# Hybrid mLSTM, attention and Fourier trunk: the gates move behind the Fourier projection, adaLN products run two blocks at a time

## The chip, the cores and the metric

The kernel runs on 1 core of one Trainium2 chip. The metric is device time in microseconds, the median of 3 runs. TensorE is called PE here, with PEld for its weight loads; VectorE is DVE, ScalarE ACT, GpSimd POOL, and SP is the engine that issues most DMAs.

## The reference, cut to what matters

Two layers work on 512 tokens (256 of context, 256 latent) of width 1024 in float32. In each layer, adaLN makes six shift, scale and gate vectors from the condition; then a mixer with three branches and a feed-forward network follow.

```python
ml = split((silu(c) @ w_ada[l] + b_ada[l]), 6)          # the same for the context: mc
h = rmsnorm(x, norm_g[l, 0]) * (1 + ml[1]) + ml[0]
u = split_cols(h @ w_in[l])   # q, k, v, o of the mLSTM; 16 gate columns; q, k, v of the attention; Fourier; merge gates
i_f, f_f, i_b, f_b = split(u[4] + gate_b, 4)            # the mLSTM's gates, per head and direction
b = cumsum(log_sigmoid(f)); dmat = where(tri, b_t - b_s + i_s, -inf); m_t = max(b_t + m, max_s dmat)
a = exp(dmat - m_t) * (q @ k.T); den = sum(a) + ...; h_ml = num / max(|den|, exp(-m_t))
y = g0 * (h_ml @ w_br_ml) + g1 * (diff_attn @ w_br_da) + g2 * (fourier @ w_br_fn)
x = x + ml[2] * (y @ w_out);  x = x + ml[5] * swiglu(modulate(rmsnorm(x), ml[3], ml[4]))
```

The gates' part (`i`, `f`, the cumulative sums and the running maximum) depends only on 16 of the projection's columns. Its results are first needed in the mLSTM, which comes after the attention.

## The kernel before, in words

**Jobs.** `plan` writes each layer as a list of jobs. A job is a piece of a weight matrix of 512 KB (128 columns by 1024 rows, or 512 by 256), used by 24 matmuls of PE. `Job.load` fetches it on SP into one of 4 raw buffers (`wraw`). `Job.split` cuts it in a high and a low part of float32r, since each product is made of three: ACT writes the high part (L214), DVE the low one by a subtraction (L224). While job i runs, `run_all` has split up to job i + 3 and asked for loads up to job i + 7, as far as raw buffers are free. `proj_t` (L309 to L311) and `proj_n` (L330 to L332) are the two kinds of matmul loop. After every sixth or so of a job's matmuls they yield: four ticks a job.

**Sides.** `side(name, gen, steps, jobs)` lets a second piece of work run along: with each tick it advances by steps / (4 x jobs) steps. `drain(name)` runs what is left of it.

**The gate job** (`GateJob`, 16 columns in a tile of 128) is loaded by a memset of POOL (L231) and four small DMAs (L233), 4 columns each. Its low part is made by POOL (L222), not DVE. Its product goes to one of the four side banks of PSUM; other projections use the four main banks.

**The gates** (`ml_gates`) are a chain on 36 partitions by 512 columns: copies from PSUM (L1015, L1018), the logarithm of the sigmoid by a polynomial of degree 12 (L1024 to L1036), two scans (L1039, L1044), copies (L1054, L1056), eight transposes on PE (L1061), and a last copy and an exponential (L1065, L1066). Nearly all of it is on DVE. It advances in 16 steps.

**adaLN** (`Ada.steps`): each of five calls multiplies the condition with 1024 rows and 2048 columns of `w_ada`, in eight blocks of 128 rows. A block is loaded by two DMAs (L364) into two of the 32 units of SBUF (`unit()`), and takes four float32 products with 32 output columns, each on its own 32 columns of PE's array; in the trace they are eight L371. In step k the loads of block k are issued, and the products of block k - 2. Two of the calls (`adab`, `adac`) run along in each layer, a fifth (`ada1`) in layer 0's feed-forward part. The opening does the same kind of product on its own (L399), two blocks together.

**Order of a layer's first part.** In layer 0 an opening of four dk jobs in a hand-written order (`opening_jobs`), in layer 1 three dk jobs (`first_jobs`). Then the gate job; then the rest of dk and dq, with the sides `gates`, `adab` and, from dq on, `hf` (the folding of the activations for the Fourier branch, `fold_h`). A rotary embedding on DVE (L1214, L1215) and POOL (L1216) takes every dk and dq block out of PSUM. Then z, the Fourier projection (`proj_z`: 8 jobs with folded weights, L789 on DVE or POOL, and L836); then dv with the side `adac`; then q, k and v with the side `da`, the attention.

**What sets the order.** SP's order is that of the program. On the other engines a planner orders the instructions when the kernel is built: it plays the program through with its own costs and takes the earliest instruction of the text that it holds to be ready. Within the opening and the layers' boundaries the order is by hand on DVE and ACT, in the opening on PE and POOL too. On the chip each engine runs its list strictly in that order.

Of the kernel before, what the change touches and what calls it, by code (L numbers as in the profile page):

```python
# [18 lines left out]
KB = D // 128  # L19
# [7 lines left out]
CQ, CK, CV, CO, CGATE, CDQ, CDK, CDV, CZ, CG = 0, 1024, 2048, 3072, 4096, 4112, 5136, 6160, 7184, 8208  # L27
# [16 lines left out]
def tile_trunk(ctx: ExitStack, tc: tile.TileContext, x, c, cx, c_ctx, w_ada, b_ada, norm_g, w_in, ml_gate_b,  # L44
               ml_head_g, da_lam, da_head_g, w_br_ml, w_br_da, w_br_fn, w_out, w_ffn_in, w_ffn_out, final_g,
               consts, out):
    nc = tc.nc
    V, S, G, T = nc.vector, nc.scalar, nc.gpsimd, nc.tensor
# [13 lines left out]
    def nm(p):  # L62
        cnt[0] += 1
        return f"{p}_{cnt[0]}"

    def unit(dt=F32):
        return upool.tile([128, 2, 512], dt, tag="u4", name=nm("u"))
# [7 lines left out]
    def main_ps():  # L75
        return pm.tile([128, 512], F32, tag="m", name=nm("m"))

    def side_ps():
        return psd.tile([128, 512], F32, tag="s", name=nm("p"))
# [15 lines left out]
    s32 = cpool.tile([128, KB, 32], F32, tag="s32", name="s32")  # L95
# [89 lines left out]
    def act_k(acts, k, n0, n1):  # L185
        return acts[0][k // 2][:, k % 2, n0:n1], acts[1][k // 2][:, k % 2, n0:n1]

    def unit_n():
        return upool.tile([128, 4, 256], F32, tag="u4", name=nm("n"))
# [46 lines left out]
    def call(fn):  # L236
        prog.append(("call", fn))

    def side(name, gen, steps, jobs):
        prog.append(("side", name, gen, steps / (4.0 * jobs)))  # L240

    def drain(name):
        prog.append(("drain", name))
# [59 lines left out]
    def proj_t(src, acts, n0, evac, cls=Job):  # L303

        def run(job):
            ps = side_ps() if cls is GateJob else main_ps()
            for k in range(KB):
                ah, al = act_k(acts(), k, n0, NT)
                T.matmul(ps[:, n0:], lhsT=job.hi[:, k, :], rhs=ah, start=(k == 0), stop=False)  # L309
                T.matmul(ps[:, n0:], lhsT=job.hi[:, k, :], rhs=al, start=False, stop=False)  # L310
                T.matmul(ps[:, n0:], lhsT=job.lo[:, k, :], rhs=ah, start=False, stop=(k == KB - 1))  # L311
                if k == KB - 1:
                    evac(ps)
                if k % 2:
                    yield
        prog.append(cls(src, KB, 128, run))

    def proj_n(src, nk, acts, tbs, evac):

        st = {}  # L320

        def mk(kt):
            def run(job):
                if kt == 0:
                    st.update({tb: main_ps() for tb in tbs})
                for tb in tbs:
                    for j in range(2):
                        k = 2 * kt + j
                        ah, al = act_k(acts(), k, tb * 128, tb * 128 + 128)
                        T.matmul(st[tb], lhsT=ah, rhs=job.hi[:, j, :], start=(k == 0), stop=False)  # L330
                        T.matmul(st[tb], lhsT=ah, rhs=job.lo[:, j, :], start=False, stop=False)  # L331
                        T.matmul(st[tb], lhsT=al, rhs=job.hi[:, j, :], start=False, stop=(k == nk - 1))  # L332
                    if kt == nk // 2 - 1:
                        evac(tb, st[tb])
                    yield
            return run
        for kt in range(nk // 2):
            prog.append(Job(src[kt * 256:kt * 256 + 256, :], 2, 512, mk(kt)))


    class Ada:
# [12 lines left out]

        def steps(self):
            self.start()
            pend = []
            for k in range(KB + 2):
                if k < KB:
                    raws = []  # L360
                    for hf in range(2):
                        raw = unit()
                        c0 = 2048 * self.s + 1024 * hf
                        nc.sync.dma_start(raw.rearrange("p a n -> p (a n)"),  # L364
                                          w_ada[self.l, k * 128:k * 128 + 128, c0:c0 + 1024])
                        raws.append(raw)
                    pend.append(raws)
                if k >= 2:
                    raws = pend.pop(0)
                    for j in range(4):  # L370
                        T.matmul(self.ps[32 * j:32 * j + 32, :], lhsT=s32[:, k - 2, :], rhs=raws[j // 2][:, j % 2, :],  # L371
                                 start=(k == 2), stop=(k == KB + 1))
                yield
            self.rows = arow_pool()
            V.tensor_tensor(out=self.rows, in0=self.ps, in1=self.bias, op=ALU.add)
            if self.s > 0:
                self.scr = dpool.tile([2, 4, 512], F32, tag="ascr", name=nm("as"))
                for r in range(2):
                    nc.sync.dma_start(self.scr[r], self.rows[r:128:32, :])
# [37 lines left out]
    def arow_pool():  # L417
        return cpool.tile([128, 512], F32, tag="arow", name=nm("ar"), bufs=3)
# [914 lines left out]
    def plan(l, xget, fin, bd1, bd2, bdn):  # L1333
# [6 lines left out]
        W = w_in[l]  # L1340
        vc = {n: vcol[:, 32 * l + o:32 * l + o + 8] for n, o in VROW.items()}
        st = {"yd": ([], []), "ym": ([], []), "q": [], "k": [], "v": [], "dq": [], "dk": [], "dv": [],
              "ys": [], "yy": ([], []), "us": ([], []), "ox": []}
        nT = len(tbs)
        hf = []
# [12 lines left out]
        h = lambda: bd1().h  # L1358
# [17 lines left out]
        def proj_tt(key, c0, nn0, rot=False, b0=0):  # L1376
            for b in range(b0, 8):
                proj_t(W[:, c0 + b * 128:c0 + b * 128 + 128], h, nn0, evac_t(key, nn0, b, rot))

        def proj_nn(key, c0, tt, f):  # L1380
            for g in range(2):
                def evac(tb, ps, g=g):
                    if tb == tt[0]:
                        st[key] += [unit_n(), unit_n()]
                    for j in range(2):
                        f(st[key][2 * g + j][:, tb, :], ps[:, j * 256:j * 256 + 256], j)
                proj_n(W[:, c0 + g * 512:c0 + g * 512 + 512], KB, h, tt, evac)
# [63 lines left out]
            opening_jobs(bd1, specs, parts)  # L1451
        else:
            first_jobs(bd1, specs)
        proj_t(W[:, CGATE:CGATE + 16], h, 0, lambda ps: st.__setitem__("gps", ps), GateJob)
        call(start)
        side("gates", lambda: ml_gates(l, st["gps"], st), 18, 10)
        side("adab", ada[1].steps, 10, 10)
        proj_tt("dk", CDK, 0, True, nop)
        side("hf", lambda: fold_h(h(), len(segs), hf, st), 12 if l == 0 else 8, 7 * nT // 4)
        proj_tt("dq", CDQ, n0, True)  # L1460
        drain("gates")
        drain("adab")
        drain("hf")
        proj_z(l, W, len(segs), hf, st)
        side("adac", ada[2].steps, 10, 8)
        proj_nn("dv", CDV, ALL, cp)
        drain("adac")
        qjobs = 8 * nT // 4
        side("da", lambda: diff_attn(l, st, tbs), (8 * nT + 4) * 3, qjobs + 15)
# [135 lines left out]
    ctx.enter_context(tc.manual_schedule(engines={mybir.EngineType.SP}))  # L1605
    call(begin)
    plan(0, None, fin, bd[0], bd[1], bd[2])
    plan(1, lambda: fin[0], fin, bd[2], bd[3], bd[4])
    run_all()

# [55 lines left out]
```

## Time and profile before

| | |
|---|---|
| runs | 1986.34, 1986.89, 1986.90 us; median 1986.89 |
| profiled execution | 1987.21 us, span 1985.4 us |
| PE busy | 1923.4 us, 97% |
| DVE busy | 1195.1 us, 60% |
| ACT busy | 783.9 us, 39% |
| POOL busy | 147.0 us, 7% |
| DMA | 269.5 MB, mean 136 GB/s |
| mean granted clock | 0.992 |

Busy time is not time at the peak: matmuls overlap, and their ends are modelled. The time that counts for PE is from start to start. Layer 0's dk and dq stand at about 61 to 157 us of the span, its z at 157 to 182 and its dv at 182 to 236; in layer 1 dk and dq are at about 1243 to 1326, z at 1326 to 1342 and dv at 1342 to 1396.

### The profile page before, as it was taken

To read this page: it belongs to the slowest core of one execution; us is meant where nothing else is said; L and a number is where in the kernel's file an instruction comes from. 1 tells how busy PE (TensorE), PEld (TensorE's weight loads), DVE (VectorE), ACT (ScalarE), POOL (GpSimd) and SP (SyncE) were. 2 spreads that over 40 slices of the span, in tenths; PEclk is the share of its full clock that TensorE was granted. 3 is DMA by queue.
4 is the path that set the end of the run, shared out by engine and by line. 5 is a ranking of instruction groups with operands and counts; after the bars stand their busy time and mean duration, and the time that the engine had idled before them with its cause. 6 is when DMAs were issued, how large, how long until landed. Compare 5 with 4: busy or idle time off the path is not lost.

```text
span 1985.4 us, 27666 instructions
## 1 busy us (share of the span) xinstructions
PE 1923.4 (97%) x10504; PEld 1586.7 (80%) x10504; DVE 1195.1 (60%) x2592; ACT 783.9 (39%) x1466; POOL 147.0 (7%) x164
## 2 busy tenths in 40 slices
PE   6999999999999999999999999989999999989998
PEld 4768688788877778888777887767878888879996
DVE  4896488852476457653333235882995477576655
ACT  3223376632343324352222224312773355335443
POOL 0240000000001110000000000250100011000000
PEclk8999999999999999999999999999999999999999
DMA  9547621224322224434443332658312564565663
GB/s 294 171 138 215 203 64 54 64 88 125 112 79 83 67 77 125 153 94 147 140 146 95 117 96 55 202 182 305 109 56 80 173 190 130 141 189 160 183 199 129
DMA packets 339895, 269.49 MB, mean 136 GB/s; under 512 B 17233, under 2 KB 296145, under 8 KB 339762
## 3 DMA queue, kind: packets, MB, share of 16 engines
q1 hardware_dynamic: 339040, 265.09, 44.1%
q10 hardware_dynamic: 722, 2.62, 0.3%
q8 instruction: 83, 1.36, 0.3%
q14 instruction: 50, 0.41, 0.1%
HBM read 264.73 MB, written 7.11 MB: 137 GB/s over the span
## 4 chain that ended last, share of the span: by engine, by line
PE 76%; DVE 14%; ACT 4%; DMA 3%; issue 2%; POOL 0%; SPq 0%; DVEq 0%; ACTq 0%; POOLq 0%
PE m L309 13%; PE m L311 12%; PE m L310 12%; PE m L330 6%; PE m L332 6%; PE m L331 6%; DVE wl L224 3%; PE p L1151 2%; DVE t L1214 2%; PE p L371 2%; PE m L567 2%; PE m L566 2%; PE m L565 2%; PE p L1115 1%; PE m L680 1%
## 5 line engine op out<-in xcount | busy, mean ns | idle before, releaser
L224 DVE TENSOR_TENSOR wl<-wr,wh 128x1024 fp32r<-128x1024 f32 x336 | 420.5, 1254 | 435.6 <-ACT wh L214 434.1
L309 PE MATMUL m<-u,wh 128*128 128x512 f32 (+1 forms) x1752 | 618.2, 353 | 1.9 <-ACT wh L214 1.9
L214 ACT CAST wh<-wr 128x1024 fp32r<-128x1024 f32 x336 | 351.7, 1050 | 672.2 <-issue 269.9
L311 PE MATMUL m<-u,wl 128*128 128x512 f32 (+1 forms) x1752 | 603.1, 344 | 1.6 <-DVE wl L224 1.6
L310 PE MATMUL m<-u,wh 128*128 128x512 f32 (+1 forms) x1752 | 602.2, 344 | 0.0
L309 PEld LDWEIGHTS m<-u,wh 128*128 128x128 f32 x1752 | 333.1, 190 | 65.9 <-issue 16.2
L311 PEld LDWEIGHTS m<-u,wl 128*128 128x128 f32 x1752 | 332.8, 190 | 41.6 <-DVE wl L224 2.7
L310 PEld LDWEIGHTS m<-u,wh 128*128 128x128 f32 x1752 | 333.1, 190 | 39.1 <-issue 4.0
L330 PE MATMUL m<-wh,u 128*128 128x512 f32 x532 | 216.1, 406 | 0.0
L332 PE MATMUL m<-wh,u 128*128 128x512 f32 x532 | 208.1, 391 | 0.0
L331 PE MATMUL m<-wl,u 128*128 128x512 f32 x532 | 207.8, 391 | 0.0
L330 PEld LDWEIGHTS m<-wh,u 128*128 128x128 f32 x532 | 100.0, 188 | 32.5 <-issue 13.6
L332 PEld LDWEIGHTS m<-wh,u 128*128 128x128 f32 x532 | 99.9, 188 | 21.3
L331 PEld LDWEIGHTS m<-wl,u 128*128 128x128 f32 x532 | 100.1, 188 | 20.3 <-issue 1.4
L1257 ACT ACTIVATE u<-p,s 128x512 f32<-128x512 f32 (+1 forms) x96 | 59.4, 619 | 39.8 <-DVE s L1256 37.6
L565 PE MATMUL m<-wh,u 128*128 128x512 f32 x180 | 70.2, 390 | 0.0
L567 PE MATMUL m<-wh,u 128*128 128x512 f32 x180 | 70.0, 389 | 0.0
L566 PE MATMUL m<-wl,u 128*128 128x512 f32 x180 | 70.0, 389 | 0.0
L1519 DVE SCALAR_TENSOR_TENSOR t<-t,m 128x512 f32<-128x512 f32 (+1 forms) x44 | 24.4, 554 | 62.7 <-PE m L311 62.1
L1254 DVE TENSOR_REDUCE s<-p 128x1 f32<-128x512 f32 (+1 forms) x96 | 57.1, 594 | 7.3 <-PE p L1252 7.1
L1214 DVE TENSOR_TENSOR t<-m,cst 32x256 f32<-32x256 f32 x128 | 53.8, 421 | 6.6 <-ACT u L1372 4.3
L1216 POOL TENSOR_TENSOR u<-u,t 128x256 f32<-128x256 f32 x32 | 43.6, 1364 | 151.7 <-DVE u L1215 139.9
(288 smaller groups left out, 2511.4 us busy)
## 6 DMA issues: line engine op xcount, KB each, us to landing
wr<-in_w_in_dram SPq DMA_DIRECT2D x176, 512.0 KB
wr<-in_w_ffn_in_dram SPq DMA_DIRECT2D x88, 512.0 KB
u<-in_w_ada_dram SPq DMA_DIRECT2D x80, 512.0 KB
wr<-in_w_ffn_out_dram SPq DMA_DIRECT2D x44, 512.0 KB
u<-in_w_ada_dram SPq DMA_DIRECT2D x32, 256.0 KB
wr<-in_w_br_da_dram SPq DMA_DIRECT2D x16, 512.0 KB
wr<-in_w_br_ml_dram SPq DMA_DIRECT2D x16, 512.0 KB
wr<-in_w_out_dram SPq DMA_DIRECT2D x16, 512.0 KB
```

The source lines that it names most:

```text
L214: S.copy(self.hi, self.raw)
L224: V.tensor_tensor(out=self.lo, in0=raw, in1=self.hi, op=ALU.subtract)
L309: T.matmul(ps[:, n0:], lhsT=job.hi[:, k, :], rhs=ah, start=(k == 0), stop=False)
L310: T.matmul(ps[:, n0:], lhsT=job.hi[:, k, :], rhs=al, start=False, stop=False)
L311: T.matmul(ps[:, n0:], lhsT=job.lo[:, k, :], rhs=ah, start=False, stop=(k == KB - 1))
L330: T.matmul(st[tb], lhsT=ah, rhs=job.hi[:, j, :], start=(k == 0), stop=False)
L331: T.matmul(st[tb], lhsT=ah, rhs=job.lo[:, j, :], start=False, stop=False)
L332: T.matmul(st[tb], lhsT=al, rhs=job.hi[:, j, :], start=False, stop=(k == nk - 1))
L565: T.matmul(ps[tb], lhsT=ah, rhs=job.hi[:, j, :], start=(k == 0), stop=False)
L566: T.matmul(ps[tb], lhsT=ah, rhs=job.lo[:, j, :], start=False, stop=False)
L567: T.matmul(ps[tb], lhsT=al, rhs=job.hi[:, j, :], start=False, stop=(k == nk - 1))
L1214: V.tensor_tensor(out=r[32 * a:32 * a + 32, :], in0=ps[src, 256:512], in1=ropes[src, :], op=ALU.mult)
```

## The change

In `Ada.steps` the products come in pairs: nothing in the even steps, and in steps 3, 5, 7 and 9 those of the two blocks i - 3 and i - 2, issued ahead of the step's loads. Each block's loads stay in their step. The gate job and its side move behind the z jobs: the chain now runs along the eight dv jobs at 18 steps for 8 jobs (it was 18 for 10), and is drained behind dv.

```diff
@@ Ada.steps
             self.start()
-            pend = []
-            for k in range(KB + 2):
-                if k < KB:
-                    raws = []
+            raws = {}
+            for i in range(KB + 2):
+                if i >= 3 and i % 2:
+
+                    for k in (i - 3, i - 2):
+                        for j in range(4):
+                            T.matmul(self.ps[32 * j:32 * j + 32, :], lhsT=s32[:, k, :], rhs=raws[k, j // 2][:, j % 2, :],
+                                     start=(k == 0), stop=(k == KB - 1))
+                if i < KB:
                     for hf in range(2):
-                        raw = unit()
+                        raws[i, hf] = unit()
                         c0 = 2048 * self.s + 1024 * hf
...
-                if k >= 2:
-                    raws = pend.pop(0)
-                    for j in range(4):
-                        T.matmul(self.ps[32 * j:32 * j + 32, :], lhsT=s32[:, k - 2, :], rhs=raws[j // 2][:, j % 2, :],
-                                 start=(k == 2), stop=(k == KB + 1))
                 yield
@@ plan
-        proj_t(W[:, CGATE:CGATE + 16], h, 0, lambda ps: st.__setitem__("gps", ps), GateJob)
         call(start)
-        side("gates", lambda: ml_gates(l, st["gps"], st), 18, 10)
         side("adab", ada[1].steps, 10, 10)
         proj_tt("dk", CDK, 0, True, nop)
         side("hf", lambda: fold_h(h(), len(segs), hf, st), 12 if l == 0 else 8, 7 * nT // 4)
         proj_tt("dq", CDQ, n0, True)
-        drain("gates")
         drain("adab")
         drain("hf")
         proj_z(l, W, len(segs), hf, st)
+        proj_t(W[:, CGATE:CGATE + 16], h, 0, lambda ps: st.__setitem__("gps", ps), GateJob)
+        side("gates", lambda: ml_gates(l, st["gps"], st), 18, 8)
         side("adac", ada[2].steps, 10, 8)
         proj_nn("dv", CDV, ALL, cp)
+        drain("gates")
         drain("adac")
```

## Rows read from the trace of the kernel before

**Rows 1.** The page: an engine's busy time and its instructions; and the chain of work that ended last, by engine.

```profile
PE 1923.4 (97%) x10504; PEld 1586.7 (80%) x10504; DVE 1195.1 (60%) x2592; ACT 783.9 (39%) x1466; POOL 147.0 (7%) x164
...
PE 76%; DVE 14%; ACT 4%; DMA 3%; issue 2%; POOL 0%; SPq 0%; DVEq 0%; ACTq 0%; POOLq 0%
```

**Rows 2.** The waits of PE over the whole span: who waited for whom, us in total, times, longest us.

```profile
PE p L1061 <- DVE u L1056: 7.2, 3, 3.8
...
PE m L814 <- DVE wl L224: 2.3, 1, 2.3
...
PE p L311 <- POOL wl L222: 1.8, 2, 0.9
...
PE p L371 <- DMA u<-in_w_ada_dram: 1.6, 4, 0.7
```

**Rows 3.** Busy time by stretch: its limits in us and its length, then each engine's busy us with its instructions, PE's granted clock, the DMA engines' mean busy share and GB/s. Layer 0's dq end, z and dv; the gate job's load in layer 1; z in layer 1; a stretch of layer 1's dv.

```profile
122.00:143.00 21.00, 16.83 (x80) 10.38 (x72) 20.59 (x40) 6.00 (x16) 5.86 (x5) 0.92 0.43 143
...
157.00:182.00 25.00, 22.70 (x203) 21.34 (x201) 19.85 (x21) 13.48 (x23) 1.65 (x1) 1.00 0.61 173
182.00:236.00 54.00, 54.00 (x262) 37.25 (x260) 15.67 (x21) 14.50 (x22) 2.42 (x3) 1.00 0.78 264
...
1204.00:1210.00 6.00, 6.00 (x28) 4.99 (x27) 1.23 (x1) 2.01 (x2) 0.00 (x0) 1.00 0.45 23
...
1326.00:1342.00 16.00, 14.88 (x136) 14.53 (x138) 11.94 (x15) 4.49 (x15) 11.22 (x5) 1.00 0.64 179
...
1350.00:1355.00 5.00, 5.00 (x24) 4.14 (x23) 0.79 (x2) 1.05 (x1) 0.00 (x0) 1.00 1.02 385
```

**Rows 4.** The chain of waits in layer 0's dk/dq stretch, in order of time: start us, us, engine and line; the last piece on DVE before PE's L1061.

```profile
131.68 1.02 DVE u L1056 x2
```

**Rows 5.** Groups of instructions by line: name, shapes and count, then busy us and mean ns of one, then the idle time before them. The first and the last of the 17 DVE groups of `ml_gates` (both layers), and its transposes on PE.

```profile
L1032 DVE SCALAR_TENSOR_TENSOR u<-u,u 36x512 f32<-36x512 f32 x24 | 18.4, 766 | 0.5
...
L1065 DVE COPY gc<-p 128x144 f32<-128x144 f32 x2 | 0.6, 303 | 0.4 <-PE p L1061 0.4
...
L1061 PE MATMUL p<-cst,u 36*128 36x36 f32 x16 | 2.2, 240 | 7.2 <-DVE u L1056 7.2
```

**Rows 6.** The timeline of PE around an adaLN block of layer 0's dk: start us, us, line, operation, count.

```profile
107.91 0.39 PE L311 MATMUL m<-u,wl 128*128 128x512 f32 x1
108.22 1.07 PE L371 MATMUL p<-u,s 128*32 128x512 f32 x8
109.22 0.50 PE L309 MATMUL m<-u,wh 128*128 128x512 f32 x1
109.56 0.39 PE L310 MATMUL m<-u,wh 128*128 128x512 f32 x1
...
114.89 1.06 PE L371 MATMUL p<-u,s 128*32 128x512 f32 x8
```

**Rows 7.** The timeline of PE in the opening, where two such blocks run together.

```profile
39.12 0.39 PE L680 MATMUL m<-u,wl 128*128 128x512 f32 x1
...
39.44 1.92 PE L399 MATMUL p<-u,s 128*32 128x512 f32 x16
41.29 1.09 PE L504 MATMUL p<-cst,u 128*128 128x128 f32 x8
```

**Rows 8.** The timeline of PE in layer 0: the first half of the first adaLN block, the last matmul ahead of L1061's wait, and the two blocks after it.

```profile
87.23 1.05 PE L371 MATMUL p<-u,s 128*32 128x512 f32 x4
...
127.91 0.39 PE L311 MATMUL m<-u,wl 128*128 128x512 f32 x1
...
132.99 1.70 PE L371 MATMUL p<-u,s 128*32 128x512 f32 x8
...
142.08 1.06 PE L371 MATMUL p<-u,s 128*32 128x512 f32 x8
```

**Rows 9.** The timeline of PE in layer 1's dq: the fourth and fifth adaLN blocks, the second half of the seventh (with the wait before it), the first piece of the eighth, and the first matmuls of z.

```profile
1288.12 1.07 PE L371 MATMUL p<-u,s 128*32 128x512 f32 x8
1292.18 1.07 PE L371 MATMUL p<-u,s 128*32 128x512 f32 x8
...
1304.83 1.05 PE L371 MATMUL p<-u,s 128*32 128x512 f32 x4 [0.20 <-DMA u<-in_w_ada_dram]
...
1315.63 1.92 PE L371 MATMUL p<-u,s 128*32 128x512 f32 x2
...
1325.80 0.39 PE L816 MATMUL m<-u,u 128*128 128x129 f32 x2
```

**Rows 10.** The timeline of all engines at the end of the opening: the gate job's first matmul, DVE's last read of the first main bank, and the split of the job after the gate job.

```profile
61.52 0.39 PE L309 MATMUL p<-u,wh 128*128 128x512 f32 x1
...
62.59 0.42 DVE L1215 TENSOR_TENSOR u<-m,cst 128x256 f32<-128x256 f32 x1
...
62.93 1.21 DVE L224 TENSOR_TENSOR wl<-wr,wh 128x1024 fp32r<-128x1024 f32 x1
```

**Rows 11.** The waits of SP's DMA queue over the whole span: the weight loads that waited for POOL's subtraction in the gate job's split.

```profile
SPq L204 <- POOL wl L222: 44.0, 2, 26.1
```

**Rows 12.** The instructions of one line: count, shortest, median and longest ns, first and last start in us. POOL's subtraction in the gate job, and the gates' first scan on DVE.

```profile
L222 POOL TENSOR_TENSOR wl<-wg,wh x2: 2381/2386/2392, 60.6 to 1246.8; 128x1024 fp32r<-128x1024 f32 x2
...
L1039 DVE TENSOR_TENSOR_SCAN u<-t,u x2: 1219/2322/3424, 110.4 to 1286.9; 36x512 f32<-36x512 f32 x2
```

**Rows 13.** The timeline in layer 0's dq: POOL's fold addition beside that scan.

```profile
108.56 4.19 POOL L757 TENSOR_TENSOR u<-u,u 128x1024 f32<-128x1024 f32 x1
```

More of the change, by code (lines that the diff above doesn't have):

```diff
@@ L356, in steps @@
             self.start()
-            pend = []
-            for k in range(KB + 2):
-                if k < KB:
-                    raws = []
+            raws = {}
[6 more added lines that the diff above has]
+                if i < KB:
                     for hf in range(2):
-                        raw = unit()
+                        raws[i, hf] = unit()
                         c0 = 2048 * self.s + 1024 * hf
[L364 to L367, printed above, removed]
-                if k >= 2:
-                    raws = pend.pop(0)
-                    for j in range(4):
-                        T.matmul(self.ps[32 * j:32 * j + 32, :], lhsT=s32[:, k - 2, :], rhs=raws[j // 2][:, j % 2, :],
-                                 start=(k == 2), stop=(k == KB + 1))
+                        nc.sync.dma_start(raws[i, hf].rearrange("p a n -> p (a n)"),
+                                          w_ada[self.l, i * 128:i * 128 + 128, c0:c0 + 1024])
                 yield
```

## The prediction

> **What bounds the kernel now.** I read the page first: PE is busy for 97% of the span and is 76% of the chain that ended last [rows 1]. So a gain has to be PE time: cheaper instructions, or less waiting. Then the waits of PE [rows 2]: the longest entry is L1061, the transposes of the gates' rows, waiting for the DVE copy L1056 (7.2 us, both layers together); L814 and the gate job's own L311 follow. Then the stretches [rows 3]: from 122 to 143 us DVE is busy for 20.59 of 21 us and PE for 16.83, at a granted clock of 0.92; in the dv stretch (182 to 236) DVE is busy for 15.67 of 54 us and PE is never idle. The chain of waits says the same: up to the stall it runs along DVE, and L1056 is its last DVE piece before PE moves [rows 4]. Layer 0's dk/dq stretch is thus bound by DVE, and the change takes DVE work out of it.
>
> **The gates' DVE work.** Its 17 groups, from L1032 to L1065, sum to 50.8 us over two layers, 25.4 a layer [rows 5]. It leaves a full stretch for one with 54 - 15.67 = 38 us of idle DVE. That idle time hides it at the new place; if it didn't fit there, it would cost PE what it costs now.
>
> *Layer 0.* From the last matmul before the stall (127.91) to the next adaLN block (142.08) pass 14.17 us [rows 8]. Undisturbed this holds 0.31 us up to the block and one step of 6.67 us from block to block [rows 6], and eight L1061 of 2.2/16 = 0.14 us [rows 5], 1.1 us: 8.1 us. So 6.1 us are lost, more than the waiting itself, because the granted clock falls behind it (the block at 132.99 lasts 1.70 us, that at 142.08 1.06). I take -6.1, bounds 0 and -6.1. L814's 2.3 us [rows 2] come from the same crowded DVE a little later: -2.3, bounds 0 and -2.3.
>
> *Layer 1.* From the block at 1292.18 to the first z matmul at 1325.80 pass 33.62 us [rows 9]. Counted in the timeline, this holds 144 half-width matmuls (six jobs of 24), four adaLN blocks and eight L1061. A step of one block and one job takes 1292.18 - 1288.12 = 4.06 us, of which the block is 1.195 (below) and the job 2.87. Undisturbed: 6 x 2.87 + 4 x 1.195 + 1.1 = 23.1; lost are 10.5 us. Up to the half block at 1304.83 I count 52 matmuls and two and a half blocks, 9.2 of 12.65 us, so 3.4 us of waiting for adaLN loads and of blocks run in halves; behind it 7.1 us, with L1061's wait and a block cut in three (1315.63). The second part goes with the gates: -7.1, bounds 0 and -7.1. Of the first I take half, -1.7 (bounds 0 and -3.4): those loads stood on SP behind weight loads that waited for DVE, but here each step wants 1.5 MB in 4 us, near the 385 GB/s that DMA reached in a stretch of the later rows [rows 3]. DMA is what is late next.
>
> **The pairs.** From the matmul before a block (107.91) to the second one after it (109.56) pass 1.65 us, from block to block, with 24 matmuls, 6.67; so a matmul is 5.02/22 = 0.228 and a block costs 1.65 - 0.455 = 1.195 us [rows 6]. The opening runs two such blocks together: from the matmul before (39.12) to the next start (41.29) pass 2.17 us [rows 7], against 109.22 - 107.91 = 1.31 for one. The second adds 0.86; a pair costs 2.055 instead of 2.39, a gain of 0.335 us. The 320 L371 are 40 blocks, 20 pairs: -6.7 us, bounds 0 (the planner pulls pairs apart) and -6.7. PE is busy at these places, so it counts in full. Layer 0's first two blocks run in halves today [rows 8], two groups too many of about 1.2 us; the first block of a pair now has one step more for its load: -1.2, bounds 0 and -2.4. The loads keep their steps and their order on SP, and no load needs a buffer that only a later product frees.
>
> **The gate job's old place.** In layer 0 the gate job wrote a side bank, so PE began it (61.52) while DVE was still emptying the opening's four main banks [rows 10]. The next job, dk's fifth block, needs a main bank: the one that L1215 reads last, until 63.01. Its own split, now on DVE (1.21 us) and ahead of that evacuation, moves this to about 64.0: a new wait of 2.5 us on PE, in place of one of 0.9 for POOL [rows 2]. +1.6, bounds -0.9 and +1.6. In layer 1 only three banks are in use there; the wait for POOL (0.9) gives way to one of about 1.1 for DVE's split behind two evacuations: +0.2, bounds -0.9 and +0.3.
>
> **Its new place.** The job's 24 matmuls cost the same 24 x 0.228 = 5.5 us, and now cover dv's loads. Its load needs a free raw buffer, POOL's memset, four small DMAs (a DMA share of 0.45 over 6 us, 2.7 us of all queues, for 64 KB [rows 3]), ACT's cast and POOL's subtraction of 2.38 us [rows 12]. In layer 0's z (22.7 us of PE, POOL almost idle) this fits. In layer 1 z is 14.9 us of PE, 1.9 a job, and its odd folds keep POOL busy for 11.22 of 16 us [rows 3]: the buffer is free some 6 us into z, then about 6 us for memset and load, 1 for the cast, 2.4 for POOL, against a need at 15 to 16; 0 to 3 us late, and 7 if the memset queues behind POOL's last fold. I take +1.5. dv's first loads stand behind this load on SP; the gate job covers them. With the chain move its four bias loads, its two stores of the rows and POOL's memsets; POOL has 2.42 of 54 us to do in dv, and these DMAs are a few KB. At the old place of the gate's load on SP, in the opening, now stands a weight load of 512 KB behind the opening's own loads: 0. L1061 still waits for DVE, but is issued at tick 29 of dv's 32, some 45 us after the chain begins, for 25 us of work: I allow +1 a layer, bounds 0 and +6.
>
> **Sum.** -6.1 - 2.3 - 7.1 - 1.7 - 6.7 - 1.2 + 1.6 + 0.2 + 1.5 + 2.0 = -19.8 us. The profiled execution took 1987.21 us (span 1985.4, and 1.8 around it), 0.3 above the median of 1986.89. 1987.2 - 19.8 = 1967.4; by the median, 1967.
>
> **A rule that speaks against it.** A row first: L1039, the same scan in each layer, took 1.22 us in one and 3.42 in the other [rows 12], and there POOL's fold addition L757 ran beside it [rows 13]. The Trainium skill (SBUF — State Buffer, Who interferes with whom) says that a DVE instruction with two SBUF inputs is locked out while GpSimd reads SBUF. This trace agrees. By that rule the gate's POOL subtraction, now inside z, would hold up DVE's folds and splits for up to its length. As a rival of its own this is 2 x 2.38 = 4.8 us more, 1972, if the hold reaches PE; I give it 0.10, as the splits run three jobs ahead.
>
> **Rivals.**
> - *The waits come back in another form* (DMA in layer 1's dq and z, L1061 in dv). For it: L371 already waits for its loads there [rows 2]. Against it: DVE has room. Left are the pairs and about 2 us of the rest; +1.6, +0.2 and +1.5 stay: 1987.2 - 6.7 - 2 + 3.3 = 1982. Chance 0.14.
> - *The gate's weights come late in layer 1*: 7 us instead of 1.5, 1973. Chance 0.10.
> - *The change doesn't do what it says*: the order on PE comes from a planner, which runs some blocks in halves already [rows 8, 9]; with the pairs pulled apart, 1967.4 + 6.7 = 1974. Chance 0.08.
> - *The other side*: the load for dv's fourth job needs the gate's raw buffer, which POOL's subtraction frees, and the adaLN loads of that stretch stand behind it on SP. SP has waited 26.1 us in one piece for just this [rows 11]; there other work covered it. Here DMA moves 264 GB/s over 54 us [rows 3], 14.3 MB, which at 385 GB/s take 37 us. With the gate job the stretch has 59.5 us, so a hold of H costs PE H + 37 - 59.5 in each layer: nothing below 22.5 us, and from 32.5 it eats the whole gain. At 36 it is 27 us, and the time 1994. Against it: POOL has 1.65 us to do in layer 0's z. Chance 0.06.
> - *All of it comes through*: loads and halves in full, no allowance, gate on time: 1967.4 - 1.7 - 1.2 - 3.5 = 1961. Chance 0.10.
>
> **How the numbers follow.** The forecast (its own range 1963 to 1972) has 0.42, the rule's 1972 0.10. A measurement of this kernel can tell about 0.2%, 4 us, from no change. Slower: the other side, and a little for orders that the planner draws anew elsewhere, 0.08. Same: the upper end of the first rival, 0.08. Faster: 0.84. The range 1957 to 1983 leaves out most of these two, and little below.
>
> **What would show it.** Right: L371 in groups of 16 of some 1.9 us; no wait of L1061 or L814; DVE well under 90% before z and near 40 of 54 us in dv; a new wait of some 2.5 us before the fifth dk block of layer 0. Wrong: groups of eight; L1061 or the gate's L311 waiting several us behind z; L371 waiting for layer 1's adaLN loads longer than its 1.6 us today; SP held behind POOL's L222.

## The result, and the profile after

The changed kernel takes 1968.18 us (median of 1965.56 to 1970.70) against 1986.62 of the kernel before on the same chip: a ratio of 0.9907, 95% interval 0.9890 to 0.9925. The forecast was 1967. The profiled execution took 1967.22 us, its span is 1965.5. In the lists below, lines behind 376 have moved up by two: the gates' transposes L1061 are L1059, the adaLN products L371 are L363, the rotation's L1214 and L1215 are L1212 and L1213, z's L814 is L812, the scan L1039 is L1037.

The page of the changed kernel, for [rows 1]: PE has 12.8 us less of busy time, and its share of the chain goes from 76% to 79%, at the cost of DVE's.

```profile
PE 1910.6 (97%) x10504; PEld 1589.3 (81%) x10504; DVE 1193.9 (61%) x2592; ACT 782.6 (40%) x1466; POOL 142.6 (7%) x164
...
PE 79%; DVE 10%; DMA 4%; ACT 4%; issue 2%; POOL 0%; SPq 0%; DVEq 0%; ACTq 0%; POOLq 0%
```

Its waits of PE (us in total, times, longest us), for [rows 2]. The 7.2 us of the gates' transposes have no line any more. A wait of 2.5 us for the rotation is new, the gate job waits for POOL once instead of twice, but longer, and z's wait is still there.

```profile
PE m L309 <- DVE u L1213: 2.5, 1, 2.5
PE m L812 <- DVE wl L224: 1.9, 2, 1.7
...
PE p L311 <- POOL wl L222: 1.7, 1, 1.7
...
PE p L363 <- DMA u<-in_w_ada_dram: 0.3, 1, 0.3
```

Busy time by stretch (columns as in [rows 3]): behind the opening, layer 0's dk and dq end, its z, and dv in layer 0 and layer 1; the last line, set apart, is the stretch behind the opening in the kernel before.

```profile
64.00:68.00 4.00, 4.00 (x12) 3.10 (x13) 3.92 (x7) 0.29 (x1) 2.32 (x2) 0.61 0.65 184
114.00:140.00 26.00, 26.00 (x130) 18.70 (x129) 24.43 (x37) 8.37 (x19) 9.11 (x6) 1.00 0.37 110
140.00:168.00 28.00, 26.02 (x220) 24.55 (x222) 23.08 (x25) 13.82 (x27) 7.54 (x5) 1.00 0.55 135
174.00:227.00 53.00, 53.00 (x267) 38.09 (x266) 36.48 (x57) 15.66 (x24) 2.82 (x4) 1.00 0.74 244
...
1326.00:1379.00 53.00, 53.00 (x267) 38.18 (x266) 35.61 (x57) 15.22 (x24) 3.82 (x4) 1.00 0.81 269
```

```profile
64.00:68.00 4.00, 4.00 (x20) 3.29 (x19) 3.87 (x9) 0.48 (x1) 2.32 (x2) 1.00 0.94 249
```

PE is now busy all through dq's end at a granted clock of 1.00, and in dv with the gates beside it DVE works 36 of 53 us. In z (140 to 168) 2 us are idle. The first row shows something new: behind the new wait the granted clock (third number from the right) is 0.61 over 4 us, where the kernel before had 1.00; its two levels, 1.2 and 2.4 GHz, are mixed in that stretch.

A pair on PE's timeline (for [rows 6, 7]): from the matmul before it to the second one behind it pass 129.68 - 127.17 = 2.51 us; less two matmuls of 0.228, the pair costs 2.05 us.

```profile
127.17 0.39 PE L311 MATMUL m<-u,wl 128*128 128x512 f32 x1
127.49 1.92 PE L363 MATMUL p<-u,s 128*32 128x512 f32 x16
129.34 0.50 PE L309 MATMUL m<-u,wh 128*128 128x512 f32 x1
129.68 0.40 PE L310 MATMUL m<-u,wh 128*128 128x512 f32 x1
```

**Where the time went.** The table takes from PE's timelines when a stage begins (the first L836 is z's end, the first L1251 the attention's start, and so on, in the lines of the kernel before), and subtracts the kernel before. The gate job's 24 matmuls (24 x 0.228 = 5.47 us) have changed stages and are taken out. "First jobs" are the first three jobs of a part, 144 matmuls and 16 transposes (L649 to L651 and L504), which run in the same order in every kernel here. The last two columns belong to the first two experiments.

| us, against before | forecast | changed kernel | pairs alone | gates alone |
|---|---|---|---|---|
| opening | 0 | -0.2 | -0.2 | -0.1 |
| layer 0, up to z's end | -9.3 | -7.8 | -0.5 | -5.5 |
| layer 0, dv | -0.3 | -0.5 | -1.3 | +0.6 |
| first jobs of layer 0's feed-forward part | 0 | 0.0 | -1.5 | 0.0 |
| the rest of that part, four pairs | -1.3 | -1.3 | -1.3 | 0.0 |
| first jobs of layer 1 | 0 | +1.5 | +1.3 | +1.3 |
| layer 1, from there up to z's end | -9.9 | -9.9 | +1.8 | -10.1 |
| layer 1, dv | +1.2 | +0.8 | -2.0 | +1.1 |
| all the rest | 0 | -2.8 | -3.3 | -1.5 |
| sum | -19.8 | -20.1 | -7.0 | -14.2 |

The two profiled executions are 20.0 us apart, the medians 18.4. So the sum came out, but not as the sum of its terms: 1.6 us less than forecast in layer 0 up to z's end, 1.5 lost in layer 1's first jobs, and 2.8 gained in the rest, the last two at places that the change doesn't touch.

### The profile page after: what moved, and what is told of

It reads as the page before. It is cut to its first block, busy times and chain, and to the rows that moved or that the text cites. A ratio compares the mean times of both kernels' runs of the same rounds, so it can differ in the third digit from the quotient of the medians.

```text
span 1965.5 us, 27681 instructions
## 1 busy us (share of the span) xinstructions
PE 1910.6 (97%) x10504; PEld 1589.3 (81%) x10504; DVE 1193.9 (61%) x2592; ACT 782.6 (40%) x1466; POOL 142.6 (7%) x164
## 4 chain that ended last, share of the span: by engine, by line
PE 79%; DVE 10%; DMA 4%; ACT 4%; issue 2%; POOL 0%; SPq 0%; DVEq 0%; ACTq 0%; POOLq 0%
PE m L309 13%; PE m L311 13%; PE m L310 13%; PE m L330 6%; PE m L332 6%; PE m L331 6%; DVE wl L224 2%; DMA wr<-in_w_in_dram 2%; PE p L1149 2%; PE m L564 2%; PE m L565 2%; PE m L563 2%; PE p L1113 1%; PE p L363 1%; PE m L678 1%
## 5 line engine op out<-in xcount | busy, mean ns | idle before, releaser
L1214 POOL TENSOR_TENSOR u<-u,t 128x256 f32<-128x256 f32 x32 | 42.5, 1327 | 327.5 <-DVE u L1213 316.3
L1212 DVE TENSOR_TENSOR t<-m,cst 32x256 f32<-32x256 f32 x128 | 53.8, 420 | 3.7 <-ACT u L1370 1.4
```

## The experiments

Every kernel ran beside the kernel before on the same chip. The last two columns are from one execution, the profiled one: when the last two matmuls of the opening began, and how long it is from there to the last row of PE's timeline, against the changed kernel's (1956.31 - 60.88 = 1895.43 us); in brackets, how much of that difference lies in the two stretches of first jobs. Why the opening and the first jobs are set apart is told with the run of the gate on DVE.

| kernel | median us | ratio to before, 95% interval | opening's end | rest (of it first jobs) |
|---|---|---|---|---|
| kernel before | 1986.62 | 1 | 61.07 | +19.9 (-1.6) |
| changed kernel | 1968.18 | 0.9907 (0.9890, 0.9925) | 60.88 | 0 (0) |
| pairs alone | 1981.09 | 0.9972 (0.9962, 0.9981) | 60.91 | +13.0 (-1.8) |
| gates alone | 1973.12 | 0.9933 (0.9918, 0.9947) | 60.98 | +5.8 (-0.3) |
| side bank, fifth dk job | 1968.60 | 0.9912 (0.9897, 0.9927) | 58.68 | +5.3 (+1.1) |
| side bank, fifth job first | 1962.39 | 0.9876 (0.9862, 0.9891) | 61.24 | -4.1 (0.0) |
| gate's low part on DVE | 1965.95 | 0.9900 (0.9885, 0.9915) | 58.86 | -1.2 (0.0) |
| gate job stays | 1967.59 | 0.9901 (0.9886, 0.9916) | 58.87 | -0.5 (0.0) |
| fold early | 1964.59 | 0.9885 (0.9868, 0.9901) | 61.61 | -3.1 (0.0) |
| groups of four | 1971.09 | 0.9920 (0.9905, 0.9935) | 61.71 | +3.6 (0.0) |
| side bank, vectors behind z | 1965.60 | 0.9896 (0.9882, 0.9911) | 58.82 | -3.5 (-0.2) |
| all three, vectors behind z | 1963.93 | 0.9888 (0.9871, 0.9904) | 60.90 | -1.1 (-0.4) |
| POOL beside the scan | 1966.17 (one execution) | | 60.51 | -0.8 (-0.4) |
| all three, vectors in place | 1958.86 | 0.9866 (0.9846, 0.9885) | 59.05 | -7.4 (-1.7) |

**Pairs alone.** The changed kernel with the gate job, the side `gates` and its drain where they were before:

```diff
+        proj_t(W[:, CGATE:CGATE + 16], h, 0, lambda ps: st.__setitem__("gps", ps), GateJob)
         call(start)
+        side("gates", lambda: ml_gates(l, st["gps"], st), 18, 10)
...
         proj_tt("dq", CDQ, n0, True)
+        drain("gates")
...
-        side("gates", lambda: ml_gates(l, st["gps"], st), 18, 8)
```

> The adaLN products in pairs, with the gates' job, their DVE work and their side schedule where the kernel before has them. If my sum is right (20 pairs at 0.335 us, and 1.2 to 2.4 us for layer 0's halves), 6.7 + 1.2 = 7.9 us are gained: about 1979. Rival, that a product gains nothing from its neighbour or that the planner pulls pairs apart: 1986 to 1987. The new 2.5 us wait for a main PSUM bank before dk's fifth block must be absent here.

Measured: 1981.09, 5.7 us less than before; 7.9 were forecast. The waits of PE, against the 7.2 us of [rows 2], say where the others stayed:

```profile
PE p L1059 <- DVE u L1054: 11.3, 2, 6.0
```

PE comes sooner to the gates' transposes and waits longer for the same DVE work: 6.0 us in layer 0 and 5.3 in layer 1. The wait before the fifth dk block is absent, as expected. In the table of stages the pairs are worth -1.3 in layer 0's dv and in the feed-forward part, where PE is the bound, and -0.5 and +1.8 up to z's end, where DVE is. The gain of a pair was right; that it counts in full beside the old gates was not.

**Gates alone.** The kernel before with the gate job, its side and its drain behind z, and each adaLN block by itself.

> The gates moved, the adaLN products one block at a time as before. My sum gives 19.8 - 7.9 = 11.9 us of gain, about 1975. If the two edits add up, the gain of this kernel and that of the pairs alone together are the whole 18.5 us or so. Rival, that the gates' move is worth nothing by itself (the stalls come back as waits for single blocks' loads): above 1982. The wait before dk's fifth block should stand here too, 2.5 us.

Measured: 1973.12, 13.7 us less. The waits of the transposes are gone, the new one stands here too (L1215, as lines haven't moved):

```profile
PE m L309 <- DVE u L1215: 2.5, 1, 2.5
```

Both gains together are 19.4 of the whole 18.4 us, so within their intervals the parts add up, though inside each stage they don't.

**A side bank for the fifth dk job.** `proj_t` gets a flag for it:

```diff
-            ps = side_ps() if cls is GateJob else main_ps()
+            ps = side_ps() if cls is GateJob or side_bank else main_ps()
...
+                       side_bank=key == "dk" and b == 4 and l == 0)
```

> The changed kernel, but layer 0's fifth dk job writes one of the two side PSUM banks instead of a main one. If the new 2.5 us wait of PE at 63.96 us is for the main bank that the copy from L1213 still reads, it goes, and with it the fall of the granted clock to 0.61 behind it: 2.5 us by the wait alone, about 4.2 us with the clock, so 1964 to 1966. Rival, that PE only meets the next late thing (DVE's splits for the sixth job) there: 1967 to 1968, with a wait of like length on a later job of that stretch.

Measured: 1968.60, no gain. PE's timeline shows the last opening matmul, the same wait, and the job in the side bank (`p`) three jobs later: the planner had changed their order, so that this run doesn't test what it was made for.

```profile
58.68 0.61 PE L678 MATMUL m<-u,wh 128*128 128x512 f32 x2
61.76 0.47 PE L309 MATMUL m<-u,wh 128*128 128x512 f32 x1 [2.47 <-DVE u L1213]
...
76.21 0.50 PE L309 MATMUL p<-u,wh 128*128 128x512 f32 x1
```

**The side bank, fifth job first.** The job now stands ahead of `call(start)`, as the gate job did before:

```diff
+        if l == 0:
+            proj_t(W[:, CDK + 512:CDK + 640], h, 0, evac_t("dk", 0, 4, True), side_bank=True)
+            nop = 5
         call(start)
```

> The run with a side bank for the fifth dk job left the wait where it was: the planner put that job three places later, so another job met the main bank. Here the same job also stands ahead of the lambda and norm vectors in the text, and PE's list begins with it. If the wait of 2.47 us is for the main bank, it goes here, the granted clock stays at 1.00 over 60 to 72 us, and the 46 matmuls behind it take 10.5 us instead of 12.2: 2.5 + 1.7 = 4.2 us, about 1964. Rival: DVE's split of that job's weights, which starts behind ACT's high part, holds PE just as long (a wait of L311 for DVE's L224 instead): 1967 to 1969.

Measured: 1962.39, 5.8 us under the changed kernel (4.1 in the traces). In its stretches the granted clock stays at 1.00 up to 72 us, and PE runs 77 matmuls in a row from 61.69 to 79.26, 17.57 us, which is 77 x 0.228. The changed kernel needs 76.21 - 60.88 = 15.33 us for 48, of which 10.94 are matmuls: the new wait cost 4.4 us, 2.5 of waiting and 1.9 of clock and restart.

```profile
60.00:64.00 4.00, 4.00 (x20) 3.20 (x19) 3.16 (x6) 4.00 (x8) 0.00 (x0) 1.00 0.19 40
64.00:68.00 4.00, 4.00 (x19) 3.34 (x18) 3.92 (x8) 1.52 (x2) 2.02 (x2) 1.00 0.69 195
68.00:72.00 4.00, 4.00 (x19) 3.30 (x19) 3.86 (x9) 0.45 (x2) 1.96 (x2) 1.00 0.57 160
72.00:88.00 16.00, 14.03 (x55) 10.93 (x54) 14.32 (x36) 2.83 (x5) 4.71 (x4) 0.89 0.73 231
```

But most of it is given back in the last of these rows: PE stands at L155, a product of two columns for the attention's lambdas, which the planner placed between two matmuls and whose DVE input comes behind four pieces of a rotation. With the clock behind it that costs 2.0 + 1.6 us. Up to z only 0.7 us are left of 4.4; the rest of the gain comes in z (-1.9) and in layer 1 (-1.0 up to dv's end, where the gate job waits 0.9 us for POOL), with the jobs drawn anew.

```profile
82.39 0.48 PE L155 MATMUL p<-s,ones 1*128 1x2 f32 x2 [1.97 <-DVE s L152]
```

**The gate's low part on DVE.** `pool = False` in `GateJob`.

> The changed kernel, but the low part of the gate job's weights is made by DVE instead of POOL. If layer 1's wait of 1.7 us (L311 for POOL's L222) is POOL's own 2.4 us and the odd folds ahead of it, it goes and about 1.7 us are gained: 1966.5. Rival by the shared-port rule (POOL's subtraction holds up DVE's folds and splits while it runs, in both layers): the gain is larger, up to 4 us. Other rival, that DVE is so full in layer 0's z that the small extra instruction costs as much there: no change.

Measured: 1965.95. In the profiled execution all of layer 0 comes 2.0 us earlier, and the whole 2.0 us arise in the opening, which no edit touches. Busy time in the opening, of the changed kernel first and of this one below, shows the same DMA rate and another granted clock, and PE gets through 23 matmuls instead of 11:

```profile
34.00:38.00 4.00, 3.98 (x11) 3.13 (x11) 3.12 (x8) 0.51 (x2) 0.00 (x0) 0.57 1.10 348
```

```profile
34.00:38.00 4.00, 4.00 (x23) 2.68 (x25) 2.71 (x8) 0.12 (x1) 0.00 (x0) 1.00 1.10 348
```

In 5 of the 14 profiles here this row reads 1.00 (not in that of the kernel before), and in just these the opening ends near 59 instead of 61 us. So 2 us of any single execution are a throw of the dice, and the last column of the table leaves them out.

The first jobs are such a place too. In all 14 profiles they are the same 160 instructions in the same order, with the same three waits of about 1.2, 0.8 and 1.8 us, and they take 24.0, some 25.4 or 26.6 us, by the granted clock behind these waits. In the feed-forward part the clock stayed at 1.00 in 4 of 14 (pairs alone, both kernels with all three, POOL beside the scan); in layer 1 only in the kernel before. Four us of layer 1's first jobs, the kernel before first and the changed one below:

```profile
1231.75:1235.75 4.00, 4.00 (x36) 4.00 (x36) 2.05 (x6) 4.00 (x10) 0.00 (x0) 1.00 0.00 0
```

```profile
1222.18:1226.18 4.00, 4.00 (x23) 4.00 (x23) 2.06 (x6) 4.00 (x10) 0.00 (x0) 0.59 0.00 0
```

By the last column the edit brings 1.2 us: nothing at all in layer 0 (-2.0 at z's start, its end and dv's end alike), and in layer 1 -1.5 up to dv's end, near the length of the gate job's wait for POOL (1.7 us), which is gone. The shared-port rival is borne out on DVE and not on PE: the split that runs beside POOL's subtraction in layer 0's z takes 2.01 us in the changed kernel (in layer 1 1.74), and with the subtraction on DVE the splits there take 1.23, but z lasts as long as in the changed kernel. The changed kernel first, then this one:

```profile
162.23 2.01 DVE L224 TENSOR_TENSOR wl<-wr,wh 128x1024 fp32r<-128x1024 f32 x1 [1.33 <-ACT wh L214]
```

```profile
159.93 1.23 DVE L224 TENSOR_TENSOR wl<-wr,wh 128x1024 fp32r<-128x1024 f32 x1
```

**The gate job stays.** `proj_t(... GateJob)` ahead of `call(start)` again, the side `gates` still beside dv.

> The gate job at its place of before, in a side bank; only the chain of the gates runs beside dv, as in the changed kernel. If the job's own move costs what the trace says (2.5 us of waiting and 1.7 us of clock in layer 0, 1.7 us at the new place in layer 1, less 0.9 of POOL's wait in each layer at the old one), this gains 5.9 - 1.8 = 4.1 us: 1964. Rival: the job covers the loads and splits of dv's first jobs at its new place, and without it they hold PE by about what is gained: 1967 to 1969.

Measured: 1967.59, no change. Layer 0 gains 2.6 us up to dv's end, as no job meets a main bank early: there the first theory holds. Layer 1 loses 1.2, and its waits of PE account for that (L814 there is L816 of the kernel before, a product of z). First the changed kernel, then this one, both in layer 1 alone; the last line is the run with the gate's low part on DVE:

```profile
PE p L311 <- POOL wl L222: 1.7, 1, 1.7
...
PE m L814 <- DVE u L787: 1.2, 2, 0.7
PE m L311 <- DVE wl L224: 1.0, 1, 1.0
...
PE p L363 <- DMA u<-in_w_ada_dram: 0.3, 1, 0.3
```

```profile
PE m L814 <- DVE u L787: 2.7, 2, 1.9
PE p L363 <- DMA u<-in_w_ada_dram: 1.9, 3, 1.1
...
PE p L311 <- POOL wl L222: 0.8, 1, 0.8
```

```profile
PE m L814 <- DVE u L787: 2.5, 2, 1.7
```

-0.9 - 1.0 + 1.5 + 1.6 = +1.2. That the job behind z is cover, as the rival has it, is shown for 0.7 us only, two waits for adaLN loads behind its place. The longer waits for folded weights (2.7 us) and the load that is 1.15 us late stand ahead of that place, in z and dq, and the run on DVE, which has the job behind z, waits 2.5 us for folded weights too. Why the changed kernel waits only 1.2 there stays open. Later stages lose another 1.1, so that 0.5 us remain.

**Fold early.** In layer 0 the side `hf` starts with the remaining dk jobs.

```diff
+        if l == 0:
+            side("hf", lambda: fold_h(h(), len(segs), hf, st), 12, 10)
         proj_tt("dk", CDK, 0, True, nop)
-        side("hf", lambda: fold_h(h(), len(segs), hf, st), 12 if l == 0 else 8, 7 * nT // 4)
+        if l == 1:
+            side("hf", lambda: fold_h(h(), len(segs), hf, st), 8, 7 * nT // 4)
```

> The changed kernel, but layer 0's fold of the activations starts with the remaining dk jobs, not with dq. If z's wait of 1.7 us (L812 for DVE's split) is the folds crowding DVE just ahead of z, it goes: 1.9 us less, 1966. Rival: the splits wait behind the fold's weights (L787), which come in z itself and don't move; then the wait stays and the time is 1968, or 1 to 2 us more if the folds now crowd the dk jobs' rotations.

Measured: 1964.59; z takes 23.2 us instead of 26.3 for the same 192 matmuls, and waits nowhere. In the changed kernel DVE makes folded weights (L787) three at a time ahead of the split that PE needs, as its list shows, and PE stands for 1.74 us until the first split of the three ends:

```profile
149.97 4.00 DVE L787 TENSOR_TENSOR u<-wr,wr 128x1016 f32<-128x1016 f32 x3
153.89 3.48 DVE L224 TENSOR_TENSOR wl<-u,wh 128x1024 fp32r<-128x1024 f32 x3
```

```profile
155.16 0.39 PE L812 MATMUL m<-u,wl 128*128 128x258 f32 x1 [1.74 <-DVE wl L224]
```

With the fold spread over ten jobs instead of seven, z's stretch reads:

```profile
140.00:168.00 28.00, 28.00 (x238) 26.55 (x237) 18.32 (x19) 12.98 (x24) 7.78 (x8) 1.00 0.64 163
```

DVE works 18.32 us there instead of 23.08, and PE is never idle.

**Groups of four.** The products of four blocks in steps 5 and 9 (`if i in (5, 9)`, `range(i - 5, i - 1)`).

> The changed kernel with adaLN products of four blocks together, in steps 5 and 9: 20 groups fewer become 10 fewer again. If the gain of a pair is a fixed cost of a change between the kinds of matmul, 0.335 us each, this gives 10 x 0.335 = 3.4 us more: 1965. Rivals: the gain belongs to the first neighbour alone: 1968; or the raw units, which stay taken four steps longer, make loads late and PE waits for them: above 1970, with a wait of L363 or of a split for DMA.

Measured: 1971.09, 2.9 us more. The price of a change is confirmed: 104.09 - 99.87 - 0.455 = 3.77 us for a group of four, 0.34 less than two pairs of 2.05, and layer 0 is 1.7 us shorter up to the attention.

```profile
99.87 0.39 PE L311 MATMUL m<-u,wl 128*128 128x512 f32 x1
100.19 3.64 PE L363 MATMUL p<-u,s 128*32 128x512 f32 x32
...
104.09 0.40 PE L310 MATMUL m<-u,wh 128*128 128x512 f32 x1
```

But in the feed-forward part the last block's load is late, PE's clock falls (0.91 over 60 us), and 9.6 us are lost there, of which later parts of layer 1 give back some. That is the second rival: SP's queue shows, over 960 to 1070 us, that adaLN loads (L369) waited for the products that free their units, 42.9 us at the longest.

```profile
1065.18 1.05 PE L363 MATMUL p<-u,s 128*32 128x512 f32 x4 [2.91 <-DMA u<-in_w_ada_dram]
```

```profile
1020.00:1080.00 60.00, 54.55 (x238) 40.61 (x236) 19.25 (x29) 13.84 (x18) 0.52 (x1) 0.91 0.31 90
```

```profile
SPq L369 <- PE p L363: 47.8, 3, 42.9
```

The Trainium skill (TensorEngine Tiling (Array Packing), Key Properties) says that changing the tiling mode drains TensorE. The rows agree with a price for each change: each group saved, whether in pairs or in fours, brought 0.34 us. What the 0.34 us consist of, no run here shows.

**The side bank, with the vectors behind z.** As the run with the job first, and in layer 0 `call(start)` stands behind `proj_z`.

> The fifth dk job first and in a side bank, and in layer 0 the norm and lambda vectors behind z instead of ahead of the rest of dk. With the side bank alone the main bank's wait was gone, but PE then stood 1.97 us at the lambda's product (L155), with a granted clock of 0.89 over 72 to 88 us. If that is a matter of where the planner puts L155 between the rotations, it goes with the move: 2.0 us and some 1.3 us of clock, 3 us less than the 1962.4 measured there, about 1959. Rival: DVE is short of time in that stretch whatever stands there, and another job waits for its split or its bank as long: 1962.

Measured: 1965.60. The first half of the forecast came: L155 doesn't wait, and z starts 4.5 us earlier than in the changed kernel, the opening taken out, which is the wait's 4.4. The second half was lost again in dv, 4.2 us between z's end and the gates' transposes. SP's list now has the vectors' five small loads ahead of dv's weights, and PE stands 1.45 us further on, for a bank that ACT empties (L1359); the first adaLN pair there runs in three pieces, and the vectors' own small products have moved there as well. Whether the small loads set this off isn't shown:

```profile
160.83 0.76 SPq L132 DMA_DIRECT2D t<-in_ml_head_g_dram  x1
...
165.73 2.65 SPq L204 DMA_DIRECT2D wr<-in_w_in_dram  x2
```

```profile
193.38 0.50 PE L330 MATMUL m<-wh,u 128*128 128x512 f32 x1 [1.45 <-ACT n L1359]
```

**All three, with the vectors behind z.**

> The side bank for the fifth dk job with the vectors behind z, layer 0's fold from the first dk job on, and the gate's low part on DVE. If the three waits are separate, their gains add to the changed kernel's 1968.2: the bank and its clock 4.2, z's wait with the fold 3.1, the gate's wait in layer 1 1.5 us (each from its own run's trace): 8.8 us, 1959.4. Rival: the earlier fold takes the DVE time that the freed jobs need, and only the larger of the two counts: 1962 to 1963.

Measured: 1963.93. Up to z's end it is 7.8 us ahead of the changed kernel; the same 4.2 us are lost in dv, and 3.1 in layer 1's mLSTM, where nothing was changed (a wait of 1.9 us for DVE, with the clock behind it).

**All three, with the vectors in place.**

> The side bank for the fifth dk job, layer 0's fold from the first dk job on and the gate's low part on DVE, with the norm and lambda vectors at their old place, so that dv's loads aren't held up. L155's wait of 2.0 us and its clock stay. Against the run with the side bank alone (1962.4), whose z still waits 0.9 us at L812 and 2.4 at L814 and whose gate job waits 0.9 for POOL in layer 1, up to 1.5 + 0.9 = 2.4 us are to be had: 1960. Rival: the fold's earlier start crowds the rotations further, and L155 or another job waits longer by as much: 1962 to 1964.

Measured: 1958.86, a ratio of 0.9866 (0.9846 to 0.9885) to the kernel before and the shortest time of all. By the medians it beats the changed kernel by 9.3 us, by the gains over the kernel before on its own chip by 8.3. Its profile holds two lucky throws, the short opening (1.8 us) and the fast first jobs (1.7). Without both it is 5.7 us ahead, 1.6 more than the side bank with the job first, where up to 2.4 were forecast. L155 still waits its 2.0 us, and z in layer 0 waits nowhere.

**POOL beside the scan.** One addition of POOL over 36 x 1024 elements, whose result nobody reads, released together with the scan:

```diff
+        busy = unit()
+        G.tensor_tensor(out=busy[R], in0=b[R], in1=b[R], op=ALU.add)
         F = gi[R, 1, :]
```

> The changed kernel plus one useless addition of POOL over 36 x 1024 elements of SBUF, in each layer, released by what releases the scan L1037 in dv. If a POOL instruction that reads SBUF is what made the scan 3.42 us instead of 1.22 in one layer of the kernel before, the scan here takes about the length of the addition, 2.4 to 4 us, in both layers. Rival: the long scan came from something else in that stretch (a DMA, the crowded queue): 1.2 us as in the changed kernel. The time itself should not move, 1966 to 1970, as DVE has 16 us to spare in dv.

Measured: 1966.17 in its one execution. The scan takes 1.21 us in the changed kernel, where no POOL work runs beside it, and 2.84 here in both layers, beside an addition of 1.89 (lines moved by two):

```profile
196.08 2.84 DVE L1039 TENSOR_TENSOR_SCAN u<-t,u 36x512 f32<-36x512 f32 x1
```

```profile
195.96 1.89 POOL L1037 TENSOR_TENSOR u<-u 36x1024 f32<-36x1024 f32 x1 [26.24 <-DVE u L1034]
```

POOL began 0.12 us earlier, and 2.84 - 1.21 = 1.63 us is about what was left of it. That accounts for the 3.42 us of [rows 12], whose addition began 1.85 us earlier and ran 2.34 us on. The Trainium skill (SBUF — State Buffer, Who interferes with whom) states it so: a DVE instruction with two SBUF inputs is shut out while a GpSimd instruction reads SBUF. This run agrees; in the time it cost nothing, since DVE has room in dv.

## Why the prediction was right, and where its terms were not

*The gates' DVE work.* Right. dv hides it: 36.5 and 35.6 us of DVE in 53, with PE never idle, and no wait of the transposes. The allowance of 1 us a layer was more than enough: the run with the gates alone shows +0.6 in layer 0, and +1.1 in layer 1, of which 0.9 are the gate job's wait for POOL. The eight transposes' own time, 0.7 us by the timeline, moved from dk and dq to dv with the chain; no term of the prediction says so.

*Layer 0.* The stall went, -6.1 and more: up to z's start 8.0 us were gained, though the new wait took more than forecast. z's 2.3 us did not go. The step that failed is "L814's 2.3 us come from the same crowded DVE a little later": they come from DVE, but from the folds and folded weights, not from the gates. The run with the early fold shows it: 3.1 us, more than the term, by an edit that leaves the gates alone.

*The gate job's old place.* The mechanism was right to a tenth: a main bank, free at 64.0, PE at 63.96. The size was not: 4.4 us instead of 2.5, because the granted clock fell behind the wait. The prediction had priced just that at the old stall (6.1 us for 3.8 of waiting) and left it out of its own term. In layer 1 the wait for DVE's split came as forecast, 0.95 us for about 1.1.

*Layer 1.* -9.9 as forecast, from the first jobs up to z's end; the 1.5 us lost in the first jobs themselves are the clock's throw told above. Inside it dk and dq gave 11.0 us, and z took 1.1 longer, for which there was no term. The loads' 1.7 came by this sum: PE's wait for them went from 1.6 to 0.3 us, though the last pair ran in three pieces, of 8, 4 and 4. The gate job waited 1.7 us for POOL where 1.5 stood in the sum, and the run on DVE got 1.5 back.

*The pairs.* 2.05 us for a pair, 2.055 forecast; four pairs in the feed-forward part -1.3, forecast -1.3, in the changed kernel and with the pairs alone. What the prediction did not see is that pairs and gates aren't separate: pairs alone make the stall longer, 11.3 us for 7.2.

*What stood in no term.* 2.8 us in the rest, nearly all of it in layer 1. Busy time in the same stretch of layer 1's mLSTM, before and after:

```profile
1570.00:1590.00 20.00, 18.41 (x119) 15.94 (x118) 9.33 (x9) 9.01 (x11) 0.00 (x0) 0.91 0.91 251
```

```profile
1553.00:1573.00 20.00, 18.59 (x132) 16.11 (x131) 10.56 (x10) 9.34 (x11) 0.00 (x0) 1.00 0.94 271
```

PE idles for about 1.5 us in both. Before, the clock falls behind it, and after, it doesn't: 1.8 us. None of the other twelve profiles has this fall either, and the first side-bank run stops there for 0.84 and 0.76 us, just as the kernel before does for 0.83 and 0.76:

```profile
1553.00:1573.00 20.00, 18.40 (x131) 15.93 (x130) 10.27 (x10) 9.33 (x11) 0.00 (x0) 1.00 0.95 270
```

So these 1.8 us are no gain of the change that the runs could show. Another 1.2 us are a wait of the Fourier merge for DVE (1.4 to 0.2 us); why it went isn't settled. The pairs alone and the gates alone have both, but the gates alone lose 1.3 us between them to a new wait for DVE, and kernels that differ elsewhere lose up to 3 us again in that stretch. That the forecast met the time within 1.2 us is therefore partly luck: in the traces it was 1.6 us short in layer 0, and at places where it claimed nothing 1.5 us were lost and 2.8 gained, most of this by the clock.

*The rivals.* SP was not held: its weight loads waited 7.1 us in all for the gate's subtraction, 3.6 at the longest, for 44.0 and 26.1 of [rows 11].

```profile
SPq L204 <- POOL wl L222: 7.1, 2, 3.6
```

Pairs were pulled apart once in 20. Of the first rival's waits, L1061 in dv did not come, and those for DMA in layer 1's dq were 0.3 us; the new waits (2.5 and 1.7 us) were in the sum, and z's 1.9 never left. The rule's hold came on DVE, 0.8 us of one split in layer 0, and did not reach PE there.

## What to carry to other kernels

Price a new wait of PE with what the clock can do behind it: here 2.5 us of waiting cost 4.4. A saving on PE ahead of a stretch that another engine bounds is spent on a longer wait there, as with the pairs beside the old gates. A job taken out of a list exposes the resource that the next job needs, a main bank here; giving that job the freed resource, and its old place in the text, won 5.8 us by the medians and 4.1 by the traces. Before two executions are compared by their traces, look for stretches that hold the same instructions and the same waits in both, and take out those in which they differ all the same: here the opening, the first jobs of two parts and a stretch of layer 1's mLSTM.

## What was not expected of the hardware

The opening, the same instructions in every kernel, has two lengths 2 us apart, with a granted clock of 1.00 or 0.57 to 0.67 in one stretch of 4 us. The first jobs of two parts, the same 160 instructions with the same waits, take 24.0, some 25.4 or 26.6 us. And a stop of some 1.5 us in all, at the same place of the program, was followed by a fall of the granted clock in one kernel (0.91 over 20 us) and by none in the others, one of which stopped just as long.
